# The feed-forward products of a decoder block by seven block products in place of eight

## The chip, the cores and the metric

The kernel runs on one core of a Trainium2 chip. The metric is the device time of one execution in microseconds, as the median of several runs. Engines: TensorE (PE) multiplies, VectorE (DVE) and ScalarE (ACT) do the elementwise work, SyncE (SP) and GpSimd (POOL) mostly issue DMAs. Each engine takes its own instructions strictly in order and waits on semaphores.

## The reference

One decoder layer for 512 tokens of width 2048: an attention branch and a gated recurrence, merged, projected by `w_out`, and then a feed-forward part with 5632 hidden values. All is float32. Cut to what matters here:

```python
y = merged @ w_out[l]
x = x + gate1 * rmsnorm(y, g_post_mix[l])

h = rmsnorm(x, g_pre_ffn[l]) * (1.0 + scale2) + shift2
gu = h @ w_ffn_in[l]                       # [512, 2048] @ [2048, 2 * 5632]
g_ffn, u_ffn = jnp.split(gu, 2, axis=-1)
y = (jax.nn.silu(g_ffn) * u_ffn) @ w_ffn_out[l]   # [512, 5632] @ [5632, 2048]
x = x + gate2 * rmsnorm(y, g_post_ffn[l])
```

## The kernel before

Every float32 product is made of three matmuls on high and low parts (`mm3`, lines 136 to 138 of the profile): high by high, high by low, low by high. A weight is loaded by SP as a tile of 128x1024 (512 KB, `wraw`, L123); ACT casts the high part (`whi`, L124), VectorE takes the difference (`wlo`, L125). Three such tiles are in flight, and a scheduler gives them a priority `ahead` of the other work, so that their casts stand early in each engine's queue.

`tblock` makes 128 weight columns by the tokens (the weight is stationary), `nunit` makes 128 tokens by 512 weight columns. `bg` is a list of generators, small chains of steps (transposes, sums) of which one step is placed between the matmuls at each `bg.tick()`. `late_ada` is such a chain: one of 16 pieces of the modulation vectors, four loads of 1 MB (`ada`, two buffers), 16 multiply-adds on VectorE (L248) into `adaacc`, and a matmul with `ones` (L656 or L665). Twelve pieces run in the merge, the last four in the feed-forward part.

After the merge, `w_out` is multiplied in two token halves. `norm1(tb)` normalises a block of 128 tokens, adds x, writes it to `x1_dram`, and normalises again; `to_h2` transposes it to h. The feed-forward part begins while that goes on: the first four hidden blocks (`up(j, hid[j], ...)`) are done for tokens 0 to 255 and again for 256 to 511. `up(hc, hid)` makes the gate block, its Silu, the other block, their product and the split. Then, for each of 11 groups of 512 hidden values, four `up` and `down` of the group before, which adds to `y2` in SBUF (L780). At the end each token block is squared, scaled by G2 and the root, added to `xr2` (two buffers) and stored.

## Time and profile before

| what | value |
|---|---|
| median of 3 runs | 2848.43 us (2845.16 to 2848.64) |
| the profiled execution's own time | 2845.16 us |
| its span | 2845.2 us, 36577 instructions |
| PE busy | 2796.0 us (98%) |
| VectorE busy | 1474.2 us (52%) |
| ACT busy | 965.8 us (34%) |
| DMA | 409.68 MB, mean 144 GB/s |

Busy times are sums over instructions; the duration of one matmul includes its passage through the array, so that the spacing of starts tells what it costs in a stream. The chain of waits follows the work that ended last back to the start.

### The profile page before, as it was taken

How to read it: one execution, taken by the hardware profiler on the slowest of the kernel's cores; microseconds unless marked ns; L12 is line 12 of the kernel's file. 1: busy time of each engine (PE TensorE's matmuls, PEld its weight loads, DVE VectorE, ACT ScalarE, POOL GpSimd, SP SyncE). 2: the span in 40 equal slices, each digit the busy share in tenths (PEclk: the TensorE clock that was granted, in tenths of full speed). 3: DMA queues.
4: the chain of work that ended last, by engine and by line, in shares of the span. 5: the costliest groups of instructions: out<-in, count | busy, mean ns of one | idle time of the engine just before them, and what ended most of it. 6: DMA issues, size and time to landing. Idle time of an engine off the chain costs nothing.

```text
span 2845.2 us, 36577 instructions
## 1 busy us (share of the span) xinstructions
PE 2796.0 (98%) x14936; PEld 2298.5 (81%) x14936; DVE 1474.2 (52%) x2398; ACT 965.8 (34%) x1457; POOL 31.2 (1%) x57
## 2 busy tenths in 40 slices
PE   6999999999999999999999999999999999999998
PEld 5777777888788888887998888888888888888887
DVE  5654559786655564856673325353333323233336
ACT  4235664664322222346642222222222222222223
POOL 0000000000000000000000000000000000000000
PEclk9999999999999999999999999999999999999999
DMA  8732222223755664666674234343333333333324
GB/s 343 306 104 84 78 76 82 79 87 111 259 199 180 217 225 156 210 200 231 224 273 135 97 96 156 96 156 96 96 96 97 97 96 97 96 97 96 97 97 140
DMA packets 98936, 409.68 MB, mean 144 GB/s; under 512 B 11664, under 2 KB 11920, under 8 KB 84176
## 3 DMA queue, kind: packets, MB, share of 16 engines
q1 hardware_dynamic: 94768, 388.53, 40.6%
q0 software_dynamic: 3856, 18.65, 1.9%
q8 instruction: 117, 1.92, 0.3%
q14 instruction: 51, 0.42, 0.0%
q10 hardware_dynamic: 144, 0.17, 0.0%
HBM read 394.72 MB, written 12.58 MB: 143 GB/s over the span
## 4 chain that ended last, share of the span: by engine, by line
PE 80%; DVE 3%; DMA 1%; ACT 1%; issue 0%; DVEq 0%; ACTq 0%
PE acc L136 26%; PE acc L137 26%; PE acc L138 26%; DMA wraw<-in_w_out_dram 1%; DVE wlo L125 1%; DVE scT L459 1%; PE bg L449 0%; ACT whi L124 0%; DVE X L415 0%; DMA wraw<-in_w_fi_dram 0%; DVE y L831 0%; DVE X L414 0%; PE bg L665 0%; PE bg L750 0%; PE bg L656 0%
## 5 line engine op out<-in xcount | busy, mean ns | idle before, releaser
L125 DVE TENSOR_TENSOR wlo<-wraw,whi 128x1024 fp32r<-128x1024 f32 x516 | 630.9, 1224 | 878.5 <-ACT whi L124 873.9
L124 ACT CAST whi<-wraw 128x1024 fp32r<-128x1024 f32 x516 | 542.9, 1053 | 1592.3 <-PE acc L137 945.4
L136 PE MATMUL acc<-ahi,whi 128*128 128x512 f32 (+1 forms) x2432 | 933.6, 384 | 1.6 <-ACT whi L124 1.6
L138 PE MATMUL acc<-ahi,wlo 128*128 128x512 f32 (+1 forms) x2432 | 921.3, 379 | 0.5 <-DVE wlo L125 0.5
L137 PE MATMUL acc<-alo,whi 128*128 128x512 f32 (+1 forms) x2432 | 921.1, 379 | 0.0
L136 PEld LDWEIGHTS acc<-ahi,whi 128*128 128x128 f32 x2432 | 458.6, 189 | 89.8 <-issue 4.3
L138 PEld LDWEIGHTS acc<-ahi,wlo 128*128 128x128 f32 x2432 | 458.2, 188 | 87.7 <-DVE wlo L125 1.0
L137 PEld LDWEIGHTS acc<-alo,whi 128*128 128x128 f32 x2432 | 458.9, 189 | 81.7 <-issue 0.5
L136 PE MATMUL acc<-whi,fhi 128*128 128x512 f32 x640 | 250.6, 392 | 0.0
L138 PE MATMUL acc<-whi,flo 128*128 128x512 f32 x640 | 249.0, 389 | 0.0
L137 PE MATMUL acc<-wlo,fhi 128*128 128x512 f32 x640 | 249.0, 389 | 0.0
L248 DVE SCALAR_TENSOR_TENSOR adaacc<-ada,first,adaacc 128x512 f32<-128x512 f32 x256 | 192.1, 750 | 77.8 <-DMA ada<-in_ada_l_dram 39.2
L136 PE MATMUL acc<-whi,ahi 128*128 128x512 f32 (+1 forms) x512 | 205.3, 401 | 4.0 <-ACT ahi L131 2.4
L138 PE MATMUL acc<-whi,alo 128*128 128x512 f32 (+1 forms) x512 | 198.7, 388 | 2.1 <-DVE alo L132 2.1
L137 PE MATMUL acc<-wlo,ahi 128*128 128x512 f32 (+1 forms) x512 | 198.1, 387 | 1.2 <-DVE wlo L125 1.0
L136 PEld LDWEIGHTS acc<-whi,fhi 128*128 128x128 f32 x640 | 120.1, 188 | 25.8 <-issue 1.0
L137 PEld LDWEIGHTS acc<-wlo,fhi 128*128 128x128 f32 x640 | 120.1, 188 | 25.7 <-issue 1.0
L138 PEld LDWEIGHTS acc<-whi,flo 128*128 128x128 f32 x640 | 120.1, 188 | 25.0
L780 DVE TENSOR_TENSOR y<-y,acc 128x512 f32<-128x512 f32 x160 | 106.4, 683 | 40.7 <-PE acc L138 40.7
L136 PEld LDWEIGHTS acc<-whi,ahi 128*128 128x128 f32 x512 | 97.3, 190 | 30.9 <-ACT ahi L131 6.5
L138 PEld LDWEIGHTS acc<-whi,alo 128*128 128x128 f32 x512 | 97.0, 189 | 25.2 <-DVE alo L132 5.5
L137 PEld LDWEIGHTS acc<-wlo,ahi 128*128 128x128 f32 x512 | 97.4, 190 | 19.1 <-DVE wlo L125 2.3
(230 smaller groups left out, 2169.3 us busy)
## 6 DMA issues: line engine op xcount, KB each, us to landing
wraw<-in_w_fi_dram SPq DMA_DIRECT2D x192, 512.0 KB, 3.6
ada<-in_ada_l_dram SPq DMA_DIRECT2D x64, 1024.0 KB, 7.0
wraw<-in_w_fo_dram SPq DMA_DIRECT2D x88, 512.0 KB, 3.5
ada<-in_ada_r_dram SPq DMA_DIRECT2D x32, 1024.0 KB, 7.5
wraw<-in_w_gate_dram SPq DMA_DIRECT2D x64, 512.0 KB, 3.7
wraw<-in_w_out_dram SPq DMA_DIRECT2D x64, 512.0 KB, 4.3
wraw<-in_w_hg_dram SPq DMA_DIRECT2D x48, 512.0 KB, 3.5
wraw<-in_w_qa_dram SPq DMA_DIRECT2D x16, 512.0 KB, 4.8
```

Source lines behind the costliest of these rows:

```text
L124: nc.scalar.copy(out=hi[:, :width], in_=raw[:, :width])
L125: nc.vector.tensor_tensor(out=lo[:, :width], in0=raw[:, :width], in1=hi[:, :width].bitcast(F32), op=ALU.subtract)
L136: nc.tensor.matmul(pt, lhsT=ahi, rhs=bhi, start=first, stop=False)
L137: nc.tensor.matmul(pt, lhsT=ahi, rhs=blo, start=False, stop=False)
L138: nc.tensor.matmul(pt, lhsT=alo, rhs=bhi, start=False, stop=last)
L248: nc.vector.scalar_tensor_tensor(out=acc[:, :width], in0=t[:, j * width:(j + 1) * width], scalar=c_sb[:, kc:kc + 1], in1=acc[:, :width], o ...
L459: nc.vector.tensor_reduce(out=sct[rows, tb, 32 * a:32 * a + 32], in_=pm[rows].rearrange("p l t -> p t l"), axis=AX.X, op=ALU.add)
L780: nc.vector.tensor_tensor(out=dst, in0=dst, in1=pt, op=ALU.add)
```

## The change

The two feed-forward products are each cut once into halves of tokens, of the inner dimension and of the columns. In place of eight products of halves there are seven, between sums and differences of the blocks (Strassen's algorithm in Winograd's form). The products are numbered 1 to 7. In the up part a group of 512 hidden values is done as seven products of four weight tiles (`up_product`), in the order 1, 5, 6, 3, 7, 2, 4; products 1 and 2 of groups 0 and 1 come first, since they need only the first token half or no sums. VectorE makes the differences of weights (`sub`, L843), ACT and VectorE then split them (`wsplit`, L136 and L137). The products come out with tokens on partitions, so `hid_turn` transposes the hidden values back on PE (16 transposes a group) and `hid_forms` makes the seven forms of the left factor for the down part; each is split into a tile `fs` (two buffers) and written to `f_dram` by POOL (512 KB). All 11 groups are done before the down part begins. That has two parts (groups 0 to 5, and 6 to 10); for each product the forms are reloaded by SP (`fa`, L1052) with the weights, 12 matmuls for each group and column half, and ACT or VectorE move the finished product to `y2` (L1068, L1070). All 16 late pieces run in the merge, one for every second block; the last four are kept in `g2_dram`. The first up products follow both `norm1` of the second half.

The core of the diff:

```diff
             else:
                 nc.tensor.matmul(pm, lhsT=ones, rhs=acc, start=True, stop=True)
                 sl = slice((i % 4) * 512, (i % 4) * 512 + 512)
-                nc.vector.tensor_tensor(out=post[:, sl], in0=post[:, sl], in1=pm, op=ALU.mult)
+                dst = post[:, sl]
+                if i >= 12:
+                    dst = pool.tile([P, 512], F32, name="g2p", tag="g2p", bufs=2)
+                    nc.gpsimd.dma_start(dst, g_post[1][:, sl])
+                nc.vector.tensor_tensor(out=dst, in0=dst, in1=pm, op=ALU.mult)
+                if i >= 12:
+                    nc.gpsimd.dma_start(g2_dram[:, sl], dst)
 
         nc.gpsimd.dma_start(G1, g_post[0])
-        pieces = iter(range(12))
+        pieces = iter(range(16))
         m1 = [mp.tile([P, S], F32, name=f"m1_{i}") for i in range(KC)]
...
-            if dc % 8 in (1, 4, 7):
+            if dc % 2:
...
-            if dc % 8 in (1, 4, 7):
+            if dc % 2:
                 bg.add(late_ada(mp, next(pieces), G1))
         bg.finish()
...
+    def to_h2_second(wait):
+        yield wait
+        for kp in range(8):
+            h0 = nb.tile([P, 2, 256], F32, name="h0", tag="h0", bufs=2)
+            nc.gpsimd.dma_start(h0, h0_dram[kp])
+            h = raw_h2(kp, 1)
+            s = nb.tile([P, 4, 256], F32, name="s", tag="s", bufs=2)
+            nc.vector.tensor_tensor(out=s[:, 0], in0=h[:, 0], in1=h[:, 1], op=ALU.add)
+            nc.vector.tensor_tensor(out=s[:, 1], in0=s[:, 0], in1=h0[:, 0], op=ALU.subtract)
+            nc.vector.tensor_tensor(out=s[:, 2], in0=h0[:, 0], in1=h[:, 0], op=ALU.subtract)
+            nc.vector.tensor_tensor(out=s[:, 3], in0=h0[:, 1], in1=s[:, 1], op=ALU.subtract)
+            split(acts[kp][0][:, 256:512], acts[kp][1][:, 256:512], s[:, 0])
+            split(fx[kp][0], fx[kp][1], s[:, 1:4])
+            neg_split(acts[kp + 8][0][:, 256:512], acts[kp + 8][1][:, 256:512], h[:, 1])
+            yield 1
...
+        if half == 1:
+            bg.finish()
+        for tb in tbs:
+            norm1(tb)
+        if half == 0:
+            bg.add(to_h2_first(24))
...
-        def down(gi, hid):
-            for n in range(4):
-                nunit(w_fo, n * (HC // 2) + gi * (GRP // 2), hid, lambda tb, pt, n=n: add_y(gi, tb, n, pt))
...
-        for gi in range(1, NGRP):
-            hid = hid_tiles()
-            for j in range(GRP):
-                up(gi * GRP + j, hid[j])
-            if 2 <= gi <= 5:
-                bg.add(late_ada(fp, 10 + gi, G2))
-            down(gi - 1, prev)
...
+    def wsplit(pool, src):
+        hi = pool.tile([P, 1024], F32R, name="bhi", tag="bhi", bufs=3)
+        lo = pool.tile([P, 1024], F32R, name="blo", tag="blo", bufs=3)
+        split(hi, lo, src)
+        return hi, lo
...
+    def weight_form(i, c, load, kept, keep):
+
...
+        if i == 5:
+            if ("t", c) not in kept:
+                kept["t", c] = load(0, 0, c, "t")
+            b = load(0, 1, c, "b")
+            sub(kept["t", c], b, kept["t", c])
+            return kept["t", c]
+        if i == 6:
+            kept["q", c] = load(1, 1, c, "b")
+            sub(kept["t", c], kept["q", c], kept["t", c])
+            return kept["t", c]
+        if i == 3:
+            return kept["q", c]
+        if i == 7:
+            b = load(0, 1, c, "b")
+            sub(b, kept["q", c], b)
+            return b
...
-            xr = fp.tile([P, 2048], F32, name="xr2", tag="ada", bufs=2)
...
+    def up_product(j, i, st, keep=True):
+        fresh = {1: "x", 5: "y", 2: "z"}.get(i, "")
+        if fresh:
+            st[fresh] = [acc_bank() for _ in range(2)]
+        bank = st[{1: "x", 6: "x", 7: "x", 4: "x", 5: "y", 3: "y", 2: "z"}[i]]
+
...
+        for c in range(4):
+            with tc.high_priority(offset=ahead[0]):
+                b = wsplit(ffs, weight_form(i, c, load, st["kept"], keep))
+            for kk in range(2):
+                mm_unit(bank, form(i, 2 * c + kk), b, kk, bool(fresh) and c == 0 and kk == 0, c == 3 and kk == 1)
+                bg.tick()
...
+        def add(t):
+            for tb in range(2):
+                nc.vector.tensor_tensor(out=t[:, tb], in0=t[:, tb], in1=bank[tb], op=ALU.add)
...
+            nc.vector.tensor_tensor(out=st["c22"], in0=st["c22"], in1=sg, op=ALU.mult)
+            bg.add(hid_forms(j, st))
...
+    def hid_forms(j, st):
...
+        def put(i, src, how=split):
+            fs = fft[0].tile([P, 2, 2, 256], F32R, name="fs", tag="fs", bufs=2)
+            how(fs[:, 0], fs[:, 1], src)
+            nc.gpsimd.dma_start(f_dram[i - 1, j], fs.bitcast(F32).rearrange("p h m t -> p (h m t)"))
...
+    for j in range(2):
+        for i in (1, 2):
+            up_product(j, i, sts[j], keep=False)
+    bg.finish()
+    rightB.close()
+    fft.append(fftx.enter_context(tc.tile_pool(name="fft", bufs=1, side="right", reuse_waits="tile")))
+    for j in range(NGRP):
+        st = sts.get(j) or group()
+        for i in ((5, 6, 3, 7, 4) if j < 2 else (1, 5, 6, 3, 7, 2, 4)):
+            up_product(j, i, st)
...
+    def finish_rows(tb):
+        ts_ = slice(tb * P, (tb + 1) * P)
+        xr = dr.tile([P, D], F32, name="xr2", tag="xr2", bufs=1)
+        nc.gpsimd.dma_start(xr, x1_dram[ts_])
+        ssum = dr.tile([P, 1], F32, name="ssum", tag="ssum", bufs=2)
+        nc.vector.tensor_reduce(out=ssum, in_=ss3[:, tb], axis=AX.X, op=ALU.add)
+        r = rstd(ssum, D, 1, dr)
+        for n in range(2):
+            sl = slice(n * 1024, (n + 1) * 1024)
+            nc.vector.scalar_tensor_tensor(out=y2[tb][:, sl], in0=y2[tb][:, sl], scalar=r, in1=xr[:, sl], op0=ALU.mult, op1=ALU.add)
+            nc.sync.dma_start(out[ts_, sl], y2[tb][:, sl])
+
+    for part, js in enumerate((range(0, 6), range(6, NGRP))):
+        kept, bank = {}, {}
+        for i in ((1, 5, 6, 3, 7, 2, 4) if part == 0 else (2, 1, 5, 6, 3, 7, 4)):
+            chain = {1: "x", 6: "x", 7: "x", 4: "x" if part == 0 else "w", 5: "y", 3: "y", 2: "z"}[i]
...
+            for j in js:
+                with tc.high_priority(offset=ahead[0]):
+                    fa = dr.tile([P, 2, 2, 256], F32R, name="fa", tag="fa", bufs=6)
+                    nc.sync.dma_start(fa.bitcast(F32).rearrange("p h m t -> p (h m t)"), f_dram[i - 1, j])
+                for cg in range(2):
...
+                    for kk in range(2):
+                        mm_unit(bank[chain][cg], (fa[:, 0, kk], fa[:, 1, kk]), b, kk, fresh and j == js[0] and kk == 0,
+                                j == js[-1] and kk == 1)
+            name = put_to[i]
+            for tb in range(2):
+                for cg in range(2):
+                    dst, src = quarter(*where[name], cg, tb), bank[chain][cg][tb]
...
+                        nc.vector.tensor_tensor(out=dst, in0=dst, in1=src, op=ALU.add)
+                    if part == 1 and i == 7:
+                        dst = quarter(1, 0, cg, tb)
+                        nc.vector.tensor_tensor(out=dst, in0=dst, in1=src, op=ALU.add)
+                if part == 1:
+                    if i == 1:
+                        finish_part(tb, 0)
+                    elif i == 3:
+                        finish_part(tb, 1)
+                        finish_rows(tb)
+                    elif i == 7:
+                        finish_part(2 + tb, 1)
+                    elif i == 4:
+                        finish_part(2 + tb, 0)
+                        finish_rows(2 + tb)
```

Where it moves instructions, three places.

VectorE at the end of the merge, before: `m` and `sgm` belong to the merge, `adaacc` to a late piece, `y` to `w_out`.

```order
L248 SCALAR_TENSOR_TENSOR adaacc<-ada,first,adaacc 128x512 x2
L696 TENSOR_TENSOR sgm<-sgm,acc 128x512
L697 TENSOR_TENSOR m_14_6898<-m_14_6898,sgm 128x512
L125 TENSOR_TENSOR wlo<-wraw,whi 128x1024
L132 TENSOR_TENSOR alo_103<-m_14_6898,ahi_102 128x512
L696 TENSOR_TENSOR sgm<-sgm,acc 128x512
L697 TENSOR_TENSOR m_15_6899<-m_15_6899,sgm 128x512
L125 TENSOR_TENSOR wlo<-wraw,whi 128x1024
L667 TENSOR_TENSOR G_6879<-G_6879,bg 128x512 x2
L132 TENSOR_TENSOR alo_105<-m_15_6899,ahi_104 128x512
L125 TENSOR_TENSOR wlo<-wraw,whi 128x1024 x7
L761 COPY y_0_10223<-acc 128x512
```

And after the change:

```order
L709 TENSOR_TENSOR m_14_6899<-m_14_6899,sgm 128x512
L130 TENSOR_TENSOR wlo<-wraw,whi 128x1024
L137 TENSOR_TENSOR alo_103<-m_14_6899,ahi_102 128x512
L708 TENSOR_TENSOR sgm<-sgm,acc 128x512
L709 TENSOR_TENSOR m_15_6900<-m_15_6900,sgm 128x512
L130 TENSOR_TENSOR wlo<-wraw,whi 128x1024
L677 TENSOR_TENSOR g2p<-g2p,bg 128x512
L246 MEMSET adaacc 128x512
L677 TENSOR_TENSOR g2p<-g2p,bg 128x512
L137 TENSOR_TENSOR alo_105<-m_15_6900,ahi_104 128x512
L253 SCALAR_TENSOR_TENSOR adaacc<-ada,first,adaacc 128x512 x16
L677 TENSOR_TENSOR g2p<-g2p,bg 128x512
```

Before, the last multiply-adds stood ahead of the last two merge blocks; now the sixteen of one more piece stand behind them, with that piece's memset.

ACT where `w_out` ends and the feed-forward part begins, before (`whi` are weight casts, `fsg` hidden values, `junk` squares, `rstd` roots):

```order
L727 ACTIVATE junk,ssq<-acc 128x512
L198 ACTIVATE rstd<-rstd 128x1
L124 CAST whi<-wraw 128x1024 x2
L714 ACT_TABLE_LOAD
L714 ACTIVATE fsg<-acc 128x256
L124 CAST whi<-wraw 128x1024
L727 ACTIVATE junk,ssq<-y_2_10225 128x512 x4
L124 CAST whi<-wraw 128x1024
L198 ACT_TABLE_LOAD
L198 ACTIVATE rstd<-rstd 128x1 x2
L124 CAST whi<-wraw 128x1024
L131 CAST fhi_10212<-fsg 128x256
```

And after (`bhi` are the weight casts of the up part):

```order
L730 ACTIVATE junk,ssq<-acc 128x512
L129 CAST whi<-wraw 128x1024 x5
L730 ACTIVATE junk,ssq<-acc 128x512 x2
L203 ACTIVATE rstd<-rstd 128x1
L730 ACTIVATE junk,ssq<-y_2_10355 128x512 x4
L203 ACTIVATE rstd<-rstd 128x1 x2
L730 ACTIVATE junk,ssq<-y_3_10356 128x512 x4
L203 ACTIVATE rstd<-rstd 128x1
L136 CAST bhi<-bq 128x1024 x6
L757 ACTIVATE h_11876<-bg,ab 128x256 x2
L908 COPY cc<-acc 128x512
L774 ACTIVATE ahi_90<-h_11876 128x256
```

The weight casts stood between the steps of the two norms; now the first of the up part stand behind the last root.

ACT where the last hidden values are made, before (`fhi` are split hidden values):

```order
L714 ACTIVATE fsg<-acc 128x512
L124 CAST whi<-wraw 128x1024 x2
L131 CAST fhi_20008<-fsg 128x512
L124 CAST whi<-wraw 128x1024 x2
L714 ACTIVATE fsg<-acc 128x512
L124 CAST whi<-wraw 128x1024 x2
L131 CAST fhi_20010<-fsg 128x512
L124 CAST whi<-wraw 128x1024 x4
L131 CAST ahi_74<-wraw 128x512
```

And after (`ht` are transposed hidden values, `sraw` sums of them, `tq` the first weights of the down part):

```order
L948 COPY ht_18460<-bg 128x512
L931 ACTIVATE cd<-acc 128x512 x2
L948 COPY ht_18460<-bg 128x512
L136 CAST fs<-ht_18460 128x512 x2
L948 COPY ht_18483<-bg 128x512 x2
L774 ACTIVATE fs<-ht_18483 128x512
L136 CAST fs<-sraw 128x512 x4
L136 CAST bhi<-tq 128x1024 x13
L1068 COPY y_0_18547<-acc 128x512
```

Weight casts stood between the hidden values; now the first cast of the down part stands behind all seven `fs`.

## Rows read from the trace of the kernel before

**Rows 1.** The page: busy time of each engine, and the chain's shares by line.

```profile
PE 2796.0 (98%) x14936; PEld 2298.5 (81%) x14936; DVE 1474.2 (52%) x2398; ACT 965.8 (34%) x1457; POOL 31.2 (1%) x57
...
PE acc L136 26%; PE acc L137 26%; PE acc L138 26%; DMA wraw<-in_w_out_dram 1%; DVE wlo L125 1%; DVE scT L459 1%; PE bg L449 0%; ACT whi L124 0%; DVE X L415 0%; DMA wraw<-in_w_fi_dram 0%; DVE y L831 0%; DVE X L414 0%; PE bg L665 0%; PE bg L750 0%; PE bg L656 0%
```

**Rows 2.** Windows: stretch, length, busy (count) by engine, PE clock, DMA share, GB/s.

```profile
0.00:60.00 60.00, 38.48 (x253) 26.55 (x254) 35.94 (x93) 28.03 (x36) 0.20 (x4) 1.00 0.98 388
1200.00:1400.00 200.00, 197.73 (x943) 164.77 (x943) 121.64 (x136) 108.98 (x170) 3.74 (x7) 0.99 0.66 218
1400.00:1500.00 100.00, 96.53 (x734) 92.65 (x734) 74.86 (x101) 55.12 (x89) 2.07 (x4) 1.00 0.75 269
1500.00:2000.00 500.00, 500.00 (x2202) 412.96 (x2201) 196.39 (x221) 111.84 (x123) 2.07 (x4) 1.00 0.36 116
```

**Rows 3.** Timeline of PE, first feed-forward blocks: start, duration, instruction.

```profile
1382.78 0.28 PE L136 MATMUL acc<-ahi,whi 128*128 128x256 f32 x1
...
1383.86 0.28 PE L136 MATMUL acc<-ahi,whi 128*128 128x256 f32 x1
...
1415.89 0.38 PE L750 MATMUL bg<-first,y 128*128 128x128 f32 x2
...
1416.83 0.38 PE L750 MATMUL bg<-first,y 128*128 128x128 f32 x2
```

**Rows 4.** Groups by shape: count, busy us, mean ns of one, idle before.

```profile
L125 DVE TENSOR_TENSOR wlo<-wraw,whi 128x1024 fp32r<-128x1024 f32 x516 | 630.9, 1224 | 878.5 <-ACT whi L124 873.9 <-PE bg L454 4.2
L124 ACT CAST whi<-wraw 128x1024 fp32r<-128x1024 f32 x516 | 542.9, 1053 | 1592.3 <-PE acc L137 945.4 <-PE acc L138 390.5 <-issue 171.2
...
L132 DVE TENSOR_TENSOR alo<-h,ahi 128x256 fp32r<-128x256 f32 x32 | 13.0, 422 | 4.0 <-ACT ahi L131 3.8
...
L727 ACT ACTIVATE junk<-y 128x512 f32<-128x512 f32 x16 | 9.9, 622 | 1.6 <-DVE y L736 1.6
...
L735 DVE SCALAR_TENSOR_TENSOR y<-y,rstd,G 128x2048 f32<-128x2048 f32 x4 | 9.4, 2350 | 0.0
L736 DVE TENSOR_TENSOR y<-y,xr 128x2048 f32<-128x2048 f32 x4 | 9.1, 2285 | 0.0
```

**Rows 5.** Timelines at the merge's end, of VectorE and of PE.

```profile
1191.43 1.53 DVE L248 SCALAR_TENSOR_TENSOR adaacc<-ada,first,adaacc 128x512 f32<-128x512 f32 x2
...
1197.87 1.88 PE L665 MATMUL bg<-adaacc,first 128*128 128x512 f32 x4
1199.19 0.80 PE L136 MATMUL acc<-whi,ahi 128*128 128x512 f32 x1
```

**Rows 6.** DMA issues: count, KB each, median us from issue to landing.

```profile
wraw<-in_w_fi_dram SPq DMA_DIRECT2D x192, 512.0 KB, 3.6
ada<-in_ada_l_dram SPq DMA_DIRECT2D x64, 1024.0 KB, 7.0
...
xr<-x_dram POOLq DMA_DIRECT2D x4, 1024.0 KB, 6.0
...
o_dram<-oT POOLq DMA_DIRECT2D x7, 256.0 KB, 2.4
...
adaacc<-in_bada_l_dram POOLq DMA_DIRECT2D x16, 2.0 KB, 2.4
```

**Rows 7.** Timelines of the end, of PE (its last matmul) and VectorE.

```profile
2835.30 0.39 PE L138 MATMUL acc<-ahi,flo 128*128 128x512 f32 x1
...
2838.80 2.74 DVE L831 SCALAR_TENSOR_TENSOR y<-y,rstd,xr 128x512 f32<-128x512 f32 x4
```

**Rows 8.** Timeline of PE behind a wait in the merge, and one window in it.

```profile
718.03 0.50 PE L136 MATMUL acc<-ahi,whi 128*128 128x512 f32 x1 [1.62 <-ACT whi L124]
...
720.16 0.63 PE L138 MATMUL acc<-ahi,wlo 128*128 128x512 f32 x1
...
723.14 0.53 PE L136 MATMUL acc<-ahi,whi 128*128 128x512 f32 x1
...
720.00:722.00 2.00, 2.00 (x7) 1.51 (x6) 1.88 (x3) 0.40 (x1) 0.00 (x0) 0.50 0.85 283
```

More of the change, by code (lines that the diff above doesn't have):

```diff
@@ new lines, in raw_h2 @@
+    def raw_h2(kp, half):
+        pt = bg_bank().rearrange("p (a t) -> p a t", a=2)
+        h = nb.tile([P, 2, 256], F32, name="h2", tag="h2", bufs=2)
+        for a in range(2):
+            k = kp + 8 * a
+            for i in range(2):
+                nc.tensor.transpose(pt[:, a, i * P:(i + 1) * P], y1[2 * half + i][:, k * P:(k + 1) * P], ident)
+        for a in range(2):
+            k = kp + 8 * a
+            nc.scalar.activation(out=h[:, a], in_=pt[:, a], func=AF.Identity, scale=ab[:, 1, 0, k:k + 1],
+                                 bias=ab[:, 1, 1, k:k + 1])
+        return h
@@ new lines, in to_h2_second @@
+    def to_h2_second(wait):
+        yield wait
+        for kp in range(8):
+            h0 = nb.tile([P, 2, 256], F32, name="h0", tag="h0", bufs=2)
[10 more added lines that the diff above has]
+            yield 1
@@ new lines, in form, with ev @@
+    def form(i, kp):
+        if i in (1, 5):
+            src, sl = acts[kp], slice(0, 256) if i == 1 else slice(256, 512)
+        elif i in (2, 4):
+            src, sl = acts[kp + 8], slice(0, 256) if i == 2 else slice(256, 512)
+        else:
+            a = {6: 0, 7: 1, 3: 2}[i]
+            return fx[kp][0][:, a], fx[kp][1][:, a]
+        return src[0][:, sl], src[1][:, sl]
+    for half in range(2):
+        tbs = (2 * half, 2 * half + 1)
+        for n in range(4):
+            def ev(tb, pt, n=n):
+                square(pt, ssq[:, 0, tb, n:n + 1])
+                nc.vector.tensor_copy(y1[tb][:, n * 512:(n + 1) * 512], pt)
+            nunit(w_out, n * 8, acts, ev, tbs)
+        if half == 1:
[4 more added lines that the diff above has]
+            bg.add(to_h2_first(24))
@@ new lines, in hid_turn @@
+    def hid_turn(st, half, hid):
+        yield 6
+        ht = fft[0].tile([P, 4, 256], F32, name=f"ht{half}", tag=f"ht{half}")
+        st["ht", half] = ht
+        for b in range(2):
+            pt = bg_bank().rearrange("p (a t) -> p a t", a=2)
+            for a in range(2):
+                for tb in range(2):
+                    nc.tensor.transpose(pt[:, a, tb * P:(tb + 1) * P], hid[:, tb, (2 * b + a) * P:(2 * b + a + 1) * P], ident)
+            nc.scalar.copy(out=ht[:, 2 * b:2 * b + 2], in_=pt)
+            yield 1
@@ new lines @@
+    bg.finish()
+    fftx.close()
+    hidx.close()
+    actx.close()
+    upx.close()
+    banks.close()
+    banks = ExitStack()
+    psum["acc"] = psum["bg"] = banks.enter_context(tc.tile_pool(name="psd", bufs=8, space=PSUM, reuse_waits="tile"))
+    dnx = ExitStack()
+    dl = dnx.enter_context(tc.tile_pool(name="dl", bufs=1, reuse_waits="tile"))
+    dr = dnx.enter_context(tc.tile_pool(name="dr", bufs=1, side="right", reuse_waits="tile"))
+    y2 = [dr.tile([P, D], F32, name=f"y2_{tb}") for tb in range(NTB)]
```

284 lines of the change are left out of this document (171 added, 113 removed).

## The prediction

> **What bounds the kernel now.** I read the page first. PE is busy for nearly the whole span and VectorE for about half of it, and the chain of waits runs through the three matmul lines for 3 x 26% [rows 1]. The windows then show how full PE is inside the feed-forward part: 2202 matmuls of 512 columns in 500 us without a gap, so one matmul takes 500 / 2202 = 0.227 us, while VectorE is busy 39% and DMA moves 116 GB/s [rows 2]. So this part costs what its matmuls cost, and whoever removes matmuls removes time, as long as PE still finds its operands. That condition is what has to be worked out: the new scheme has fewer matmuls, more VectorE work, more DMA, and places where PE stands behind another engine's queue. The sum is made against the profiled execution (span 2845.2 us, its own time 2845.16 us), which is the lowest of the three runs; the median is 0.1% above it.
>
> **What the change takes away.** A group's up product falls from 384 to 336 matmuls (7 block products of 4 x 12), which is 11 x 48 = 528; the down product falls from 2112 to 7 x 22 x 12 = 1848, which is 264. Together 792 x 0.227 = **-179.8 us**. The first four hidden blocks were done in two token halves with 256-column matmuls, of which nine are issued in 1.08 us [rows 3], 0.12 us each; 768 of them become 384 whole ones, 768 x 0.12 - 384 x 0.227 = **-5.0 us**. Added on PE are 16 transposes a group that turn the hidden values. In the stream of the first up products two transposes and six half-wide matmuls repeat every 0.94 us [rows 3], so two cost 0.94 - 6 x 0.12 = 0.22 us: 176 x 0.11 = **+19.4 us**. Without one new wait the kernel would come to 2845.2 - 165.4 = 2679.8 us.
>
> **VectorE and DMA in the up phase.** A group now gives VectorE 28 low parts and 16 differences of 128x1024 at 1.224 us [rows 4] (53.9), and about 20 passes of 512 columns at 0.7 us, taken between 0.42 (256 columns) and 1.22 (1024): 68 us. PE needs 336 x 0.227 + 16 x 0.11 = 78 us. VectorE is then 87% busy, and three buffers of split weights cover bursts. I take +1 us for each of nine groups, **+9** (0 to 4 each: at the upper end every burst of 12 weight tiles with differences, 35.7 us of VectorE against 32.6 of PE, shows whole), and **+5** for groups 0 and 1, whose 20 units behind the shared start hold 57 us of VectorE against 54 (0 to 12). DMA reads 20 x 512 KB and writes 7 x 512 KB a group, 180 GB/s; in the down phase 197 tiles of 512 KB in 419 us, 246 GB/s. The kernel has moved 269 GB/s with PE busy for 96.5 of 100 us, and 388 at its start [rows 2], so I take nothing for bandwidth.
>
> **The merge's end.** All 16 late pieces now run in the merge. The first order rows of VectorE show the last piece's 16 multiply-adds (L253) behind the evacuation of the merge's last product, and PE must consume that piece before it starts w_out. Before, the multiply-adds ended 5 us ahead and PE lost nothing but the two pieces' own matmuls, 1.3 us [rows 5]. Now, counted from the last merge matmul: evacuation, a low part, a scaling and the memset, 2 x 0.7 + 1.2 + 0.7 + 0.5 = 3.8; the bias row, 2.4; then four 1 MB tiles of four steps at 0.75 each with two buffers, the third tile asked for after 3 us and landing 6 to 7 us later (7.0 in the median [rows 6]), the fourth by 12 us, end at 15. Total 21, of which about 1 was there: **+20** (15 to 25).
>
> **The start of the up phase.** ACT's first weight cast (L136) now stands behind the norm of token block 3, squares and root included; before, casts and half-token products were woven between [the second order rows]. PE then waits for copies 1.4, two passes each of 2.35 and 2.29, four squares of 0.62 [rows 4], roots and reductions about 2, a cast 1.05: 16 us, less what starts before the last w_out matmul, **+15** (12 to 18). Then the second token half is turned: per pair of k blocks VectorE does six passes of 256 columns at 0.42 [rows 4] and one of 768 at 0.95 (between 0.42 and 1.22), 3.5 us, eight pairs 28 us, and the weights' low parts 5; PE has 8 x (6 x 0.227 + 4 x 0.11) = 14 us of its own there and two pairs of buffers (7 us): **+11** (6 to 18).
>
> **PSUM.** Product 2 of group 1 needs banks whose adds (L913) stand on VectorE behind a later weight's low part, about 6 us; product 5 of group 0, and product 4 of groups 0 and 1, wait for two adds on the bank just finished, 1.4 us each: **+10** (6 to 15).
>
> **Between the phases.** ACT's first down cast stands behind all seven forms of the last group [the third order rows]. The forms share two buffers (fs), and each buffer is free when its 512 KB have landed in DRAM. A form takes a cast 0.6, a low part 0.7, an issue 0.5 and a landing; the trace has no 512 KB write, the nearest are 2.4 us for 256 KB and 3.6 for a 512 KB read [rows 6], I take 3.5. So two forms go every 5.3 us, the seventh cast starts 16 us after the first, and Silu, product, transposes and copies ahead of it (4.5) and the weight's cast (1.05) make 22; PE has nothing else: **+21** (15 to 27, with landings of 2.4 and 5).
>
> **Inside the down phase** VectorE has 2.45 us of work for a unit of 2.72 and runs ahead, but in part two three products start late. Product 5's first weight stands on SP behind a reload of a form (L1052) that waits for the last matmul of product 1: load 3.6, difference 1.2, cast 1.05, low part in part, 7 us. Product 7's stands so behind product 3, with four adds and two scalings on VectorE besides, 10 us. Product 4's differences stand behind eight adds and two scalings of product 7, 8 x 0.7 + 2 x 1.2 + 1.2, 9 us: **+26** (15 to 32).
>
> **The end.** Now the last matmul ends at 2835.7, the last row's four steps begin 3 us later [rows 7], and the span ends 9.5 us after the matmul. After the change two token blocks finish together, and the one buffer xr2 lets the reload for block 3 (1 MB, 6.0 us [rows 6]) start only when block 2 has used it: adds 2.7, square and scalings 3.7, root 1, block 2's row 2.45, reload 6, row 2.45, store 2.5 to 3, 21 us: **+11** (9 to 13).
>
> **The clock.** PE waited 1.6 us at 718 us, and seven matmuls from 720.16 to 723.14 started 0.43 us apart in place of 0.227, at a granted clock of 0.50 [rows 8], the lower level (1.2 GHz): with the next, eight matmuls lost 8 x 0.2 = 1.6 us. In the first 60 us, however, PE is busy for 38.5 us only and the clock stands at 1.00 [rows 2]. I charge 1.6 for each of the eight long waits above, **+13** (0 to 16). The Trainium skill says on its page "TensorE: Matmul & The Clock Gate", section "Part 1: The HAM clock gate", that an idle array falls back to 1.2 GHz and has to be busy again before it is given 2.4; by that the sum is as I have it, and without it 13 us lower. The row at 720 us agrees with it, the first 60 us don't.
>
> **Sum.** Waits 20 + 15 + 11 + 10 + 5 + 9 + 21 + 26 + 11 + 13 = +141; with -165.4 it makes -24: 2845.2 - 24 = **2821 us**, faster by 0.9%. All lower ends together (15 + 12 + 6 + 6 + 0 + 0 + 15 + 15 + 9 + 0 = 78) give 2758, all upper ends (25 + 18 + 18 + 15 + 12 + 36 + 27 + 32 + 13 + 16 = 212) 2892.
>
> **Rivals.**
> - *The waits are mostly hidden.* The order of a queue says who stands behind whom, not that he is late; if engines run further ahead than I think, the lower ends hold: 2758. For it speaks that PE was idle for only 49 of 2845 us [rows 1] under similar queues; against it that the merge's end, the two phase borders and the end have no other work for PE at all. Chance 0.20.
> - *The forms' ring stalls every group* (the other side). The casts of the seven forms stand in ACT's queue among the weight casts, and each from the third on waits for a write two before it. At 5.3 us for two forms the ring needs 18.6 us of a group of 78, and forms are one to two units (2.7 to 5.4 us) apart, so it should fit. If a write takes 7 us in place of 3.5, two forms need 8.8 us, 4.4 each, and where they stand one unit apart ACT loses 1.7; with VectorE's low parts behind it about 8 us a group: 2821 + 9 x 7 = 2884. It decides the sign from 1 + 24 / 9 = 3.7 us a group on. Chance 0.20.
> - *DMA bounds the down phase.* It reads 246 GB/s on the mean; if reloads from DRAM and weights together reach only the 218 GB/s that the stretch of w_out moved [rows 2], 103 MB take 474 us in place of 419: 2821 + 55 = 2876. But there nothing asked for more, and the 388 at the start speak against it. Chance 0.05.
> - That fewer matmuls are issued is certain from the order of PE (11190 rows in place of 12324); the change can't do nothing.
>
> **Numbers.** 2821 us has 0.55, its own range 2786 to 2856 (terms wrong by a quarter of the waits); the rivals 0.20, 0.20 and 0.05. The 80% range leaves out half of each rival that ends it: 2760 to 2880. What a measurement can tell here is about 0.2% (three runs spread over 0.12%), 5.7 us. Slower by more than that are the two slow rivals, 0.25; within it lies the top of the first case, 0.10; faster is the rest of it and the fast rival, 0.65.
>
> **What would show it.** PE's idle time by windows: one gap of some 20 us where w_out starts, one of 15 us at the first block product, a ragged stretch of 30 us behind it, 21 us between the phases with ACT in L136 fs casts, gaps of 7 to 10 us in front of products 5, 7 and 4 of the second part. Matmuls elsewhere 0.227 us apart, and a granted clock of 0.50 behind each gap. In the up phase VectorE near 87%. Wrong I am if PE waits inside every group of the up phase (second rival: waits of ACT's L136 fs on f_dram), if the gaps are absent (first), or if PE waits for DMA throughout the down phase (third).

## The result and the profile after

The changed kernel takes 2875.31 us (median of 4 runs, 2871.53 to 2876.86) against 2848.31 for the kernel before (4 runs): ratio 1.0098 [1.0084, 1.0113], slower by 1.0% where 0.9% faster was forecast. The profiled execution took 2875.33 us, 30.2 more than that of before; the spans of the two traces, from which everything below is read, are 2873.6 and 2845.2 us, 28.4 apart. Of e2_before_shift, a run below, one execution of four (3819 us at a granted clock of 0.687) is left out.

The page, the row that answers to [rows 1] (busy time of each engine), and the DMA issues of the forms, as in [rows 6]:

```profile
PE 2699.9 (94%) x13936; PEld 2156.4 (75%) x13936; DVE 2001.0 (70%) x2841; ACT 1239.8 (43%) x1759; POOL 85.1 (3%) x158
```

```profile
f_dram<-fs POOLq DMA_DIRECT2D x77, 512.0 KB, 3.1
fa<-f_dram SPq DMA_DIRECT2D x77, 512.0 KB, 3.5
```

PE's busy time fell by 96 us only, not by the 165.4 that the matmuls were to give. What PE waited for (line, releaser: us in all, times, longest):

```profile
PE acc L885 <- ACT bhi L136: 67.4, 6, 24.0
PE bg L671 <- DVE adaacc L253: 20.5, 1, 20.5
PE bg L298 <- DMA ada<-in_ada_r_dram: 18.4, 2, 17.1
PE acc L886 <- DVE blo L137: 12.0, 6, 7.1
PE acc L885 <- DVE cc L913: 6.8, 2, 5.0
PE bg L754 <- ACT h L757: 4.5, 2, 2.4
PE acc L885 <- DVE cd L913: 3.8, 3, 2.7
```

The third row belongs to the kernel's start. The others stand where waits were forecast, but for most of the fourth row (7.1 of 12.0 us), a second wait at the start of the up phase. The windows of after (columns as in [rows 2]), with one at the merge's end and one behind the wait at the start of the up phase:

```profile
1000.00:1100.00 100.00, 100.00 (x435) 80.66 (x434) 71.51 (x93) 21.33 (x24) 1.45 (x3) 1.00 0.70 246
1213.00:1233.00 20.00, 1.05 (x3) 0.19 (x1) 14.66 (x22) 0.84 (x2) 2.16 (x4) 0.60 0.60 213
...
1640.00:2300.00 660.00, 660.00 (x2936) 538.06 (x2935) 539.12 (x529) 341.19 (x404) 30.83 (x58) 1.00 0.53 177
...
2400.00:2500.00 100.00, 100.00 (x428) 80.40 (x427) 77.82 (x67) 44.11 (x48) 0.00 (x0) 1.00 0.69 248
```
```profile
1453.00:1456.00 3.00, 2.89 (x7) 2.31 (x8) 2.33 (x3) 0.00 (x0) 0.00 (x0) 0.50 1.03 411
```

And two of these stretches in the kernel before, the merge and, at the time of the other kernel's down phase, a piece of its feed-forward part:

```profile
1000.00:1100.00 100.00, 100.00 (x451) 82.95 (x450) 59.43 (x76) 21.94 (x24) 1.46 (x3) 1.00 0.56 194
...
2400.00:2500.00 100.00, 100.00 (x443) 82.81 (x442) 30.90 (x32) 24.07 (x27) 0.00 (x0) 1.00 0.30 96
```

Two things are to be seen. First, from 1640 to 2300 us PE never waits, so the forms' ring stalls nothing, and VectorE is busy 539 / 660 = 82%. Second, in stretches where PE is just as full and the clock stands at 1.00, fewer matmuls fit into 100 us: 428 in place of 443 in the down phase, and 435 in place of 451 in the merge (of 512 columns 427 in place of 435), whose products the change doesn't touch. Each matmul takes longer. In the timeline of PE the step from start to start is 0.22 to 0.23 us where the forms fx are the stationary operand (first rows), and 0.23 to 0.24 with the reloaded forms fa (second rows; start, duration, instruction). The rows have two decimals; the mean steps are 0.2270 and 0.2343 us:

```profile
1690.01 0.39 PE L885 MATMUL acc<-bhi,fxh 128*128 128x512 f32 x1
1690.23 0.39 PE L886 MATMUL acc<-blo,fxh 128*128 128x512 f32 x1
```
```profile
2500.48 0.39 PE L887 MATMUL acc<-bhi,fa 128*128 128x512 f32 x1
2500.71 0.40 PE L885 MATMUL acc<-bhi,fa 128*128 128x512 f32 x1
```

### The profile page after: what moved, and what is told of

Read it like the earlier page. It is cut to its first block, busy times and chain, and to the rows that moved or that the text cites. A ratio compares the mean times of both kernels' runs of the same rounds, so it can differ in the third digit from the quotient of the medians.

```text
span 2873.6 us, 35969 instructions
## 1 busy us (share of the span) xinstructions
PE 2699.9 (94%) x13936; PEld 2156.4 (75%) x13936; DVE 2001.0 (70%) x2841; ACT 1239.8 (43%) x1759; POOL 85.1 (3%) x158
## 5 line engine op out<-in xcount | busy, mean ns | idle before, releaser
L136 ACT CAST bhi<-bq 128x1024 fp32r<-128x1024 f32 x374 | 393.4, 1052 | 499.2 <-PE acc L887 462.5
L137 DVE TENSOR_TENSOR blo<-bq,bhi 128x1024 fp32r<-128x1024 f32 x374 | 456.1, 1223 | 186.6 <-ACT bhi L136 183.8
L129 ACT CAST whi<-wraw 128x1024 fp32r<-128x1024 f32 x244 | 255.7, 1049 | 584.5 <-PE acc L142 395.3
L130 DVE TENSOR_TENSOR wlo<-wraw,whi 128x1024 fp32r<-128x1024 f32 x244 | 298.1, 1223 | 194.8 <-ACT whi L129 189.8
L141 PE MATMUL acc<-ahi,whi 128*128 128x512 f32 x896 | 366.8, 409 | 1.8 <-ACT whi L129 1.8
L143 PE MATMUL acc<-ahi,wlo 128*128 128x512 f32 x896 | 355.4, 397 | 0.4 <-DVE wlo L130 0.4
L142 PE MATMUL acc<-alo,whi 128*128 128x512 f32 x896 | 355.1, 396 | 0.0
L885 PE MATMUL acc<-bhi,ahi 128*128 128x512 f32 x704 | 285.9, 406 | 31.5 <-ACT bhi L136 20.9
L885 PE MATMUL acc<-bhi,fa 128*128 128x512 f32 x616 | 248.6, 404 | 46.5 <-ACT bhi L136 46.5
L843 DVE TENSOR_TENSOR bq<-bq 128x1024 f32<-128x1024 f32 x198 | 240.2, 1223 | 43.9 <-DMA bq<-in_w_fi_dram 35.8
L887 PE MATMUL acc<-bhi,fa 128*128 128x512 f32 x616 | 247.2, 401 | 0.0
L141 PEld LDWEIGHTS acc<-ahi,whi 128*128 128x128 f32 x896 | 169.2, 189 | 44.2 <-issue 5.0
```

Of the source, the lines that this page charges most:

```text
L129: nc.scalar.copy(out=hi[:, :width], in_=raw[:, :width])
L130: nc.vector.tensor_tensor(out=lo[:, :width], in0=raw[:, :width], in1=hi[:, :width].bitcast(F32), op=ALU.subtract)
L136: nc.scalar.copy(out=hi, in_=src)
L137: nc.vector.tensor_tensor(out=lo, in0=src, in1=hi.bitcast(F32), op=ALU.subtract)
L141: nc.tensor.matmul(pt, lhsT=ahi, rhs=bhi, start=first, stop=False)
L142: nc.tensor.matmul(pt, lhsT=ahi, rhs=blo, start=False, stop=False)
```

## The experiments

**Theories.** A: the address at which an operand starts in a partition sets the matmul's step. The change moves the activations (ahi, alo) to the other end of the memory by one line:

```
-    actp = ctx.enter_context(tc.tile_pool(name="actp", bufs=1))
+    actp = actx.enter_context(tc.tile_pool(name="actp", bufs=1, side="right"))
```

In the compiled program of before the activations start at multiples of 512 bytes, in that of after 480 past one; the reloaded forms fa start 352 past one, while fx, which keeps its step, and the split weights stand on multiples. (The traces hold no addresses. These are of the compiled programs, and each padding below moves them by its own size.) B: the other engines' and the DMA's traffic slows PE (VectorE is busy 70% of the span in place of 52). C: the right end of the memory is slower. Beside these stand the waits, which edits of order and buffers should take away.

**e1_align**: the changed kernel with 32 bytes in front of the activations.

```
+    padr = ctx.enter_context(tc.tile_pool(name="padr", bufs=1, side="right"))
+    padr.tile([P, 8], F32, name="padr")
     actp = actx.enter_context(tc.tile_pool(name="actp", bufs=1, side="right"))
```

> The changed kernel with one unused tile of 32 bytes put at the upper end of the buffer, so that the tiles on the right side (the activations acts, and the reloaded forms fa) begin at multiples of 64 bytes, where in the changed kernel they begin 32 bytes past one. Theory A: a matmul is slower when one operand begins 32 bytes past a multiple of 64. Then the 512-column matmuls that read acts or fa start 0.227 to 0.228 us apart in place of 0.233 to 0.234, some 7700 of them by 0.006 us, and the kernel takes 2875 - 48 = about 2827 us. Rival B: it is the right side, the upper half of the buffer, that is slow; then the spacing stays at 0.233 to 0.234 and the time within 5 us of 2875. Rival C: the whole chip runs slower while VectorE, ACT and DMA are busier; then too nothing changes.

Measured: 2864.09 us, ratio to before 1.0061 [1.0046, 1.0076]; 11 us came back, not 48. The activations now start 448 past a multiple of 512, fa 320. As moving operand the activations still step by 0.2332 us, as stationary operand in the products of the up phase by 0.2290 in place of 0.2332. So 64 bytes isn't the unit, or A is wrong.

**e2_before_shift**: the kernel before, with 32 bytes in front of everything from the activations on; there is no other edit.

```
+    pada = ctx.enter_context(tc.tile_pool(name="pada", bufs=1))
+    pada.tile([P, 8], F32, name="pada")
     actp = ctx.enter_context(tc.tile_pool(name="actp", bufs=1))
```

> The kernel before with one unused tile of 32 bytes in front of the activations, so that acts and every tile behind it on the left side begin 32 bytes past a multiple of 64, with no other change; the weights whi and wlo stay where they were. Theory A: all 10700 three-pass matmuls have one operand that begins 32 bytes off, 0.005 to 0.006 us each, 2848 + 55 to 65 = 2903 to 2913 us. Rival B (the right side): the tiles stay on the left and low, so 2848 us. Rival C (activity): 2848 us.

Measured: 2905.97 us (three executions), ratio 1.0208 [1.0191, 1.0225]. The window that held 443 matmuls in the kernel before:

```profile
2400.00:2500.00 100.00, 100.00 (x430) 80.44 (x429) 35.37 (x41) 21.46 (x23) 0.00 (x0) 1.00 0.31 95
```

430 matmuls, near the 428 of the changed kernel, with VectorE at 35% (31 in the kernel before) and DMA at 95 GB/s (96), on the left side of the memory. B and C fall, and an effect of addresses stands: 32 bytes cost the kernel before 2%.

**e3_waits**: the changed kernel with the late pieces spread over the merge, three buffers for the forms (and, in a line not shown, two in place of three for the sums that they are made of), two for the last rows' reload, and the reloads of forms issued by POOL.

```
-            if dc % 2:
+            if dc % 3 != 1:
...
-            if dc % 2:
+            if dc % 2 == 0 and dc < 10:
...
-            fs = fft[0].tile([P, 2, 2, 256], F32R, name="fs", tag="fs", bufs=2)
+            fs = fft[0].tile([P, 2, 2, 256], F32R, name="fs", tag="fs", bufs=3)
...
-        xr = dr.tile([P, D], F32, name="xr2", tag="xr2", bufs=1)
+        xr = dr.tile([P, D], F32, name="xr2", tag="xr2", bufs=2)
...
-                    nc.sync.dma_start(fa.bitcast(F32).rearrange("p h m t -> p (h m t)"), f_dram[i - 1, j])
+                    nc.gpsimd.dma_start(fa.bitcast(F32).rearrange("p h m t -> p (h m t)"), f_dram[i - 1, j])
```

> The changed kernel with four waits taken away, addresses left as they are: the late pieces are spread so that the last ends well ahead of the merge's end; three fs buffers in place of two (and two of its raw sums in place of three); the reloads of the forms issued by POOL in place of SP; two xr2 buffers. By my terms: the wait at the merge's end goes (21 us), the gap between the phases shrinks from 24 to about 19, the gaps of 8 us in front of products 5 and 7 of the second part go or shrink to 2 to 4, the end shrinks by 6 to 7, and the clock's loss behind each: 2875 - 45 = 2830 us. Rival: the waits stand elsewhere as soon as one is gone (VectorE full in the merge, POOL's issues later than SP's), then above 2860.

Measured: 2842.89 us, ratio 0.9981 [0.9972, 0.9990], 32 us less than the changed kernel. The wait at the merge's end is gone, the time from the last matmul to the end fell from 19.7 to 13.7 us, and the gap between the phases from 24.0 to 16.6. That one has another cause now, the reload queued on POOL behind the writes of the forms:

```profile
PE acc L885 <- DMA fa<-f_dram: 16.6, 1, 16.6
```

But in front of products 5, 7 and 4 of part two 6.1, 6.5 and 6.9 us stayed, of 7.5, 7.6 and 8.0. The order of SP, which the prediction blamed for the first two, was gone with the reloads, so it made at most 1.4 us of each.

**e4_both**: e1_align's bytes and e3_waits' edits.

> Both together: the 32-byte tile and the four waits. If the two causes add, 2875 - 48 - 45 = 2782 us, 2.3% under the kernel before; if the aligned matmuls only uncover VectorE in the up phase (70% busy now over the span, 83% in a group), less is gained there and the time is 2795 to 2810.

Measured: 2824.72 us, ratio 0.9931 [0.9915, 0.9948]. 18 us less than e3_waits: what the 32 bytes give is again a part of 48 only, though more than the 11 us that they gave alone.

**e5_align512**: the changed kernel with the activations and fa at multiples of 512.

```
+    padr.tile([P, 120], F32, name="padr")
...
-    ss3 = dr.tile([P, NTB, 2], F32, name="ss3")
+    ss3 = dr.tile([P, NTB, 32], F32, name="ss3")[:, :, 0:2]
...
-        ssum = dr.tile([P, 1], F32, name="ssum", tag="ssum", bufs=2)
+        ssum = dr.tile([P, 56], F32, name="ssum", tag="ssum", bufs=2)[:, 0:1]
```

> The changed kernel with unused bytes so that acts and fa begin at multiples of 512 bytes, as every operand of the feed-forward matmuls did in the kernel before (moving them to multiples of 64 gave 11 us of the 48 expected, and left acts as the moving operand at 0.233 us). Theory A2: a matmul reaches 0.227 us only when both operands begin at a multiple of a larger unit, up to 512 bytes. Then acts and fa come down from 0.230 to 0.234 to 0.227 to 0.228, and the kernel takes about 2875 - 48 = 2827 us. Rival B: what the multiple of 64 did not bring is due to the right side; then about 2864 us as with multiples of 64.

Measured: 2836.69 us, ratio 0.9962 [0.9947, 0.9976], 38.6 less than the changed kernel, from padding alone. The down phase holds 439 matmuls in 99.34 busy us, 0.2263 each, with more VectorE and DMA than in the changed kernel:

```profile
2400.00:2500.00 100.00, 99.34 (x439) 81.93 (x438) 85.16 (x76) 42.31 (x45) 0.00 (x0) 1.00 0.72 253
```

**e7_before_128_256** asks for the unit: the kernel before with the activations 128 bytes past a multiple of 256, and everything behind them moved by 256.

```
+    pada = ctx.enter_context(tc.tile_pool(name="pada", bufs=1))
+    pada.tile([P, 32], F32, name="pada")
     actp = ctx.enter_context(tc.tile_pool(name="actp", bufs=1))
+    padb = ctx.enter_context(tc.tile_pool(name="padb", bufs=1))
+    padb.tile([P, 32], F32, name="padb")
```

> The kernel before with acts 128 bytes past a multiple of 512, and the tiles behind them on the left (the merge's bhi and blo, the hidden values fhi and flo) 256 bytes past one. Theory A2 with a unit of 512: every three-pass matmul has an operand off the unit and starts every 0.233 us, about 2905 us as with 32 bytes. Unit of 256: only the matmuls with acts are slow, some 8000 by 0.006: 2895 us. Unit of 128, or an effect of the right side: 2847 us.

Measured: 2888.89 us, ratio 1.0144 [1.0129, 1.0159]; at 128 past it is slow, at 256 fast. The groups of PE by shape (count, busy us, mean ns of one), of the kernel before, then e2_before_shift, then this one; a group with the activations as moving operand and one with fhi, the hidden values, as stationary operand of each:

```profile
L137 PE MATMUL acc<-alo,whi 128*128 128x512 f32 x2176 | 848.7, 390 | 0.0
...
L137 PE MATMUL acc<-wlo,fhi 128*128 128x512 f32 x640 | 249.0, 389 | 0.0
```
```profile
L139 PE MATMUL acc<-alo,whi 128*128 128x512 f32 x2176 | 859.8, 395 | 0.0
...
L139 PE MATMUL acc<-wlo,fhi 128*128 128x512 f32 x640 | 253.1, 395 | 0.0
```
```profile
L141 PE MATMUL acc<-alo,whi 128*128 128x512 f32 x2176 | 859.7, 395 | 0.0
...
L141 PE MATMUL acc<-wlo,fhi 128*128 128x512 f32 x640 | 249.0, 389 | 0.0
```

Before, both are fast; 32 bytes past, both are slow; here the activations alone, 128 past, are slow, and fhi, a multiple of 256 away, is as before. The runs that change addresses and the two kernels together, as the mean step from start to start of neighbouring 512-column matmuls (steps between 0.20 and 0.26 us, each figure the mean over three lines), with the operand's start past a multiple of 256 bytes:

```
                     activations, moving   stationary              fhi or fa, stationary
kernel before          0     0.2271          0    0.2281 (w_out)     0   0.2267
changed kernel         224   0.2331          224  0.2332 (up)        96  0.2343
e1_align               192   0.2332          192  0.2290 (up)        64  0.2333
e2_before_shift        32    0.2333          32   0.2331 (w_out)     32  0.2333
e5_align512            0     0.2279          0    0.2274 (up)        0   0.2268
e7_before_128_256      128   0.2331          128  0.2323 (w_out)     0   0.2268
```

In this table the other operand, a weight, always stands on a multiple. One more group has none there: for the last products the kernel before splits weights into the tiles of the activations (ahi, alo) and multiplies them with fhi. In e2_before_shift both operands stand 32 past (first row), in e7_before_128_256 one stands 128 past and the other on a multiple (second row):

```profile
L139 PE MATMUL acc<-alo,fhi 128*128 128x512 f32 x64 | 24.9, 389 | 0.0
...
L141 PE MATMUL acc<-alo,fhi 128*128 128x512 f32 x64 | 25.3, 395 | 0.0
```

Both 32 past is as fast as both on a multiple: 0.2268 us a step over the 192 matmuls of three such groups, where e7_before_128_256 has 0.2333. So theory A is too narrow. What fits all these rows is that the distance between the two starts counts, and that a multiple of 256 is fast. Counted from the stationary operand's start to the moving one's, e1_align then has the distance 192 twice, slow both times (activations moving 0.2332, fa stationary 0.2333), and 64 once, nearly fast (0.2290). No run was made to test this; it rests on one group in one trace.

**e6_align_waits_late**: e5_align512 and e3_waits' edits, and the adds of a down product (evacuate holds the loop that stood behind the product) put behind the first group of the next one.

```
+                if pending:
+                    evacuate(*pending.pop())
+            pending.append((i, bank[chain]))
```

> The changed kernel at multiples of 512 with the four waits taken away, and with the evacuation of each down product placed behind the first group of the next product, so that VectorE makes the differences of the next product's first weights before it empties PSUM. Theory: against the 2825 us of multiples of 64 with four waits, the rest of the address cost goes (about 2450 matmuls with acts moving by 0.006, 1850 with fa by 0.007, 28 us), and the three gaps of 6 to 7 us in the second part shrink to 1 to 3 with the slow clock behind them (15 us): 2825 - 28 - 15 = 2782 us. Rival (the gaps are made by the loads, the right side is slow): 2815 to 2825.

Measured: 2789.27 us, ratio 0.9793 [0.9776, 0.9809]. Of the gaps of 6 us and more inside part two only one of 6.5 us, in front of product 4, is left; those of products 5 and 7 are 0.9 and 1.2.

**e9_late_sp**: e6_align_waits_late with the reloads of forms back on SP (the line of e3_waits undone); one execution.

> The version of 2789 us with the reloads of the forms back on SP: it tells what made the gaps in front of products 5, 7 and 4 of the second part. If it is SP's order (the next product's first weight behind a reload that waits for the last matmul), the gaps of products 5 and 7 come back at 5 to 7 us. If it is VectorE's order (evacuation and scalings ahead of the differences), they stay under 2 us, as with the reloads on POOL. The gap between the phases tells the same of the ring of fs: with three buffers and SP it is set by ACT alone, 13 to 19 us.

Measured: 2785.91 us. The gaps of products 5 and 7 are 1.9 us each, of product 4 6.1, and the one between the phases 17.9, with ACT as the releaser again. SP's order in part two costs about 1 us a product; the rest in front of products 5 and 7 was VectorE's, which stood in the adds and scalings while the next product's differences waited.

**e8_first**: e6_align_waits_late with product 1 of groups 0 and 1 issued ahead of the two norms of the second token half, and the first reloads of the down phase on SP.

```
+            sts = {j: first_product(j) for j in range(2)}
         for tb in tbs:
...
-        for i in (1, 2):
-            up_product(j, i, sts[j], keep=False)
+        up_product(j, 2, sts[j], keep=False)
```

> The version before (multiples of 512, four waits away, late evacuation: 2789 us) with product 1 of groups 0 and 1 issued ahead of the two norms of the second token half, with the staging tiles that w_out used, and the first reloads of the down phase issued by SP again. Theory: 22 us of matmuls then cover the norms, so that the 27 us in front of the first block product fall to below 8, and the gap between the phases falls from 15.5 to 10 to 13: 2789 - 22 - 3 - 2 of slow clock = 2762 us. Rival (PE waits for VectorE as soon as it reaches the second half's transposes, so the wait only moves there): 2775 to 2785.

Measured: 2781.90 us, ratio 0.9769 [0.9752, 0.9785], the best version, 2.3% faster than before, but 7 us better than e6_align_waits_late instead of 27. The gap at the start fell from 27 to 10 us, and another took its place at 1464 us:

```profile
PE acc L813 <- DVE cc L927: 20.3, 2, 15.1
```

VectorE has the same list to work off there, the second half's sums and splits: it is busy without a break from 1455 us on, and the add that PE waits for starts at 1478.76. So most of the wait moved. The gap between the phases, which was to fall to 10 to 13 us, is 18.5.

## Why the prediction was wrong, point by point

**The step that failed is the price of a matmul**: "Matmuls elsewhere 0.227 us apart". That the change would leave the 0.227 of [rows 2] as it is was taken as given. By the table above the step became 0.0060 us longer for 2688 matmuls with moving activations, 0.0051 for 1440 with stationary activations in w_out and the first projections, 0.0062 for 2112 of the up products with stationary activations and 0.0073 for 1848 with fa (against fx): 16.1 + 7.3 + 13.1 + 13.5 = 50 us, of which nearly half (16.1 + 7.3) is in the first projections, the merge and w_out, whose products are the same as before. e2_before_shift shows the cause without the change, e5_align512 that the change can be had without it. That 2875 us lies inside the forecast's 80% range of 2760 to 2880 is luck: without this term the measured ones come to about 2825.

**The account.** Term by term, with the gain of -165.4 taken as predicted and the waits as measured in the trace of after (excess of the step from one start to the next):

```
                           predicted   measured
merge's end                   20         20.5
start of the up phase         15         27.7
second token half             11          4.8
PSUM                          10         11.7
groups 0 and 1, the nine      14          0
between the phases            21         24.3
products 5, 7, 4 of part two  26         28.9
the end                       11         10.2
clock                         13         14
long steps at the full clock   0          3
sum                          141        145
slower matmuls                 0         50
with -165.4                  -24        +30     (spans of the traces: +28.4)
```

So the waits, on which most of the working went, come out at 145 for 141, though three terms are far off and their errors cancel. PE's busy time agrees: 165.4 less, and 50 + 17 more for slower matmuls, is 98 less (96.1 on the page).

- *The merge's end, the end, PSUM*: right in place and size. At the merge's end VectorE does the last piece in two pairs of tiles with a load between, as the prediction had it, where [rows 5] show it 5 us ahead:

```profile
1220.24 6.26 DVE L253 SCALAR_TENSOR_TENSOR adaacc<-ada,first,adaacc 128x512 f32<-128x512 f32 x8 [3.04 <-issue]
1228.22 6.29 DVE L253 SCALAR_TENSOR_TENSOR adaacc<-ada,first,adaacc 128x512 f32<-128x512 f32 x8 [1.71 <-DMA ada<-in_ada_l_dram]
```

- *The start of the up phase*: the mechanism is right, the term of 15 was mis-sized, 27.7. PE's rows, and VectorE's that end the second wait:

```profile
1424.98 0.40 PE L143 MATMUL acc<-whi,alo 128*128 128x512 f32 x1
1445.20 0.79 PE L885 MATMUL acc<-bhi,ahi 128*128 128x512 f32 x1 [19.82 <-ACT bhi L136]
1453.11 0.80 PE L886 MATMUL acc<-blo,ahi 128*128 128x512 f32 x1 [7.12 <-DVE blo L137]
1453.71 0.63 PE L887 MATMUL acc<-bhi,alo 128*128 128x512 f32 x1
1454.13 0.63 PE L885 MATMUL acc<-bhi,ahi 128*128 128x512 f32 x1
```
```profile
1450.64 1.29 DVE L745 TENSOR_SCALAR y<-y,rstd 128x2048 f32<-128x2048 f32 x1 [6.22 <-DMA x_dram<-y]
1451.84 3.49 DVE L137 TENSOR_TENSOR blo<-bq,bhi 128x1024 fp32r<-128x1024 f32 x3
```

  ACT's first weight cast did stand behind the norms, for 20 us. But one matmul later PE waits again: the first low part stands on VectorE behind the last scaling of y, which overwrites what a store is still reading. This second wait, 7.7 us, was in no term.
- *The second token half and the groups*: priced too high, 4.8 for 11 and nothing for 9 + 5. The buffers in front of PE covered all bursts.
- *Between the phases*: right in sum, 24.3 for 21, by two errors that cancel. ACT's rows, in which each cast of fs waits for the write two before it:

```profile
2356.55 1.14 ACT L136 CAST fs<-ht 128x512 fp32r<-128x512 f32 x2
...
2366.53 0.63 ACT L774 ACTIVATE fs<-ht 128x512 fp32r<-128x512 f32 x1 [7.41 <-DMA f_dram<-fs]
2369.05 0.62 ACT L136 CAST fs<-sraw 128x512 fp32r<-128x512 f32 x1 [1.88 <-DMA f_dram<-fs]
2376.02 0.62 ACT L136 CAST fs<-sraw 128x512 fp32r<-128x512 f32 x1 [6.35 <-DMA f_dram<-fs]
2378.51 0.62 ACT L136 CAST fs<-sraw 128x512 fp32r<-128x512 f32 x1 [1.87 <-DMA f_dram<-fs]
2380.84 0.62 ACT L136 CAST fs<-sraw 128x512 fp32r<-128x512 f32 x1 [1.71 <-DMA f_dram<-fs]
2381.36 2.94 ACT L136 CAST bhi<-tq 128x1024 fp32r<-128x1024 f32 x3
```

  The seventh cast starts 24 us after the first where 16 was worked out (a pair every 9.5 to 10 us at first, in place of 5.3): from 2350 to 2385 us a write of a form lands 7.7 us after its issue in the median, not 3.5, while the first loads of the down phase bring the DMA to 380 GB/s (2357 to 2382 us).

```profile
f_dram<-fs POOLq DMA_DIRECT2D x7, 512.0 KB, 7.7
```

  But the first cast starts before PE's last transposes (2357.36 us), where the prediction put 4.5 us of Silu, transposes and copies in front of it.

- *Inside part two*: the sum is right, 28.9 for 26, one cause isn't. Products 5 and 7 were put down to a weight behind a reload on SP; e3_waits took the reloads off SP and nearly all of the gaps stayed, e9_late_sp left them there and moved the adds, and the gaps went. VectorE in front of product 5:

```profile
2677.33 1.39 DVE L1070 TENSOR_TENSOR y<-y,acc 128x512 f32<-128x512 f32 x2 [1.42 <-PE acc L887]
2679.24 2.36 DVE L1028 TENSOR_TENSOR y<-y,G 128x1024 f32<-128x1024 f32 x2 [0.51 <-ACT bq L1027]
2682.88 1.23 DVE L843 TENSOR_TENSOR tq<-bq,tq 128x1024 f32<-128x1024 f32 x1 [1.29 <-DMA bq<-in_w_fo_dram]
```

  The adds (L1070) and scalings (L1028) run until 2681.6; the first difference (L843) starts 1.3 us later, when its weight has landed; that 1.3 us is about what SP's order costs by e3_waits and e9_late_sp. For product 4 the prediction named VectorE; the deferral left 6 us there, whose cause stays open.
- *The clock*: right in kind. Behind each long wait matmuls start 0.42 to 0.43 us apart (the timeline above) at a granted clock of 0.50 (the window at 1453 us), the lower level. After 1180 us the steps of 0.3 to 0.5 us in such stretches exceed 0.227 by 14.6 us together, 1.0 in the kernel before: 14 for 13. (Steps of that length at the full clock make 6.4 us, and 3.0 in the kernel before; the prediction has no term for them.) The rule cited from the Trainium skill's page "TensorE: Matmul & The Clock Gate", section "Part 1: The HAM clock gate", agrees with these rows. The prediction held the first 60 us against it, where [rows 2] give a clock of 1.00. That was a misreading: the clock records of that trace begin at 30.5 us, and a stretch without a record reads as 1.00. PE's rows of the kernel before show the lower level until then, steps of 0.43 us, and 0.23 behind it:

```profile
29.57 0.63 PE L137 MATMUL acc<-wlo,ahi 128*128 128x512 f32 x1
30.00 0.63 PE L138 MATMUL acc<-whi,alo 128*128 128x512 f32 x1
...
31.18 0.39 PE L136 MATMUL acc<-whi,ahi 128*128 128x512 f32 x1
31.41 0.39 PE L137 MATMUL acc<-wlo,ahi 128*128 128x512 f32 x1
```
- *The end's reload*: the last row's step waited 6.64 us for the single buffer's reload, as the prediction had it, where [rows 7] show none:

```profile
2858.02 2.48 DVE L1039 SCALAR_TENSOR_TENSOR y<-y,rstd,xr 128x1024 f32<-128x1024 f32 x2
...
2867.21 2.48 DVE L1039 SCALAR_TENSOR_TENSOR y<-y,rstd,xr 128x1024 f32<-128x1024 f32 x2 [6.64 <-DMA xr<-x_dram]
```

**The rivals.** The ring: a write took 3.1 us in the median of all 77, and no group stalled; the sign went to its side for another reason. Hidden waits: excluded by the gaps. DMA in the down phase: excluded, since e5_align512 moved 253 GB/s there with matmuls of 0.2263 us.

**What stays open.** From the changed kernel to e5_align512 the steps of the table give 14.0 + 7.2 + 12.2 + 13.9 = 47 us, the profiled spans differ by 36.9. Three of the missing 10 are matmuls at the lower clock (17.3 against 14.6 us), the rest isn't assigned. Why the start of an operand changes the step, and whether the distance between two starts is the rule, is open too.

## What to carry to other kernels

A change that moves buffers can change the price of every matmul that reads them: after one, count matmuls per full window in a stretch that the change does not touch, before any wait is looked for. Keep the starts of both matmul operands at multiples of 256 bytes, which was fast in every case here; small tiles in front of them (sums, scalars) can be why they aren't. A block scheme that saves matmuls pays with pipelines that drain at each of its borders; here 165 us were to be saved and about 145 were lost, most of it there, and spreading late work, one more buffer and deferred adds brought back 47 of them (e5_align512 to e6_align_waits_late).
